# A hybrid encoder block on one core: a hand-set TensorE order for the SSD stage, with the z projection two groups wide

## The chip, the cores and the metric

One core of one Trainium2 chip runs the whole block for one sequence. The time is device microseconds of one execution, as the median of several. Five engines run side by side, each through its own instructions in order: TensorE (PE; its weight loads, PEld, overlap the matmuls), VectorE (DVE), ScalarE (ACT), GpSimd (POOL) and SyncE (SP, which here only issues transfers; its queue stands in the trace as SPq).

## The reference

One layer on x of 512 tokens by 1024, all float32:

```python
h = rms_norm(x)
q, k, v, z, xbc, dt_raw, gates = split(h @ w_in)
attn = diff_attention(q, k, v) @ w_attn_out
ssd = bi_ssd(xbc, dt_raw, z) @ w_ssm_out
x = x + (sigmoid(gate_attn) * attn + sigmoid(gate_ssd) * ssd) @ w_out
x = x + conv_glu(rms_norm(x))
```

The part in question is `bi_ssd`. It works on xBC after a depthwise convolution over 4 tokens and SiLU, in 8 groups of 4 heads of 64 columns, with a state of 128, forward and backward, in chunks of 128 tokens:

```python
acs = cumsum(dt * a)                              # within a chunk; backward from the end
decay = exp(where(mask, acs[l] - acs[s], -inf))
y = (C B^T * decay) @ (x * dt) + exp(acs) * (C @ state)
state = state * exp(acs[-1]) + B^T @ (x * dt * exp(acs[-1] - acs))
y = rms_norm((y_fwd + y_bwd + d_skip * x) * silu(z))     # per group of 256 columns
```

## The kernel before

Every large product is made of three passes over halves: `mm3` (L200) multiplies high by high, high by low and low by high, so a matmul of 128 rows of K is three instructions (L201, L202, L203). The halves `whi` and `wlo` of a weight are made on the chip: the `raw` tile comes by a transfer that SP issues (L133), ACT casts it (L149 for row chunks, L169 for column chunks), and DVE subtracts (L150, L170). `feat` makes features by tokens, 512 tokens wide, so its instructions have 512 columns. `token` makes tokens by features, and for the gate z it is 256 columns wide: one group's z, 4 blocks of 128 tokens, 8 blocks of K, three passes.

The program runs through attention (to about 300 us), the SSD stage (to about 850 us), the output projection and the convolutional MLP. In the attention stage the order on PE is written by hand; `dt_part` (L388 to L447) makes the time step there as fill. It leaves the step `dtk`, the negated sum `acs`, `eacs`, `elast` and `wst` in tokens by heads, and the sums in DRAM as `acsD`.

The SSD stage is emitted by `weave` (L276): `ssd_group(g)`, a generator of five parts, is interleaved with fill, and from what is emitted a scheduler puts each engine's instructions in order. The fill for group g is `ssd_prep(g + 1)`, and for even g from 2 on one part of the output projection, `ssm_out` (L860), behind it. After the loop come the last `base` steps (DVE, transfers) and `ssm_out(3)`.

`ssd_prep(g)` projects B, C and the two halves of x (`feat`), each through `conv_silu` (L709: ACT L711, DVE L712 to L714, ACT tanh L716, DVE L717); turns B into tokens (L729) and makes C B^T (L734), turns x into tokens (L748), and makes the gate z (ACT L754, DVE L755). `ssd_group(g)` does:

- Six contributions to the state, in four turns: POOL weighs x with `wst` (`xw`, L775), PE multiplies (L779, plain float32, bank "av"), and DVE carries the state from chunk to chunk, four heads at a time (L787, L802), or ACT copies it (L790, L792, L795).
- Then four chunks. The row sums of both directions are spread over the partitions by a transfer on SP's queue (`E`, L809, 512 KB). POOL masks them (L813), ACT takes the exponent, 8 heads and directions (L817), ACT scales the backward half by the step (L821), DVE scales the forward half and adds (L822, into `W`), and DVE multiplies with C B^T (L823). POOL starts y with the skip (L825). PE multiplies W with x (L830) and C with the state (L834), DVE adds both (L836, L841) and the gate (L843), ACT sums the squares (L845).
- At the end of the group DVE makes the reciprocal root (L113 to L119) and scales y (L848), PE transposes it (L853), and ACT and DVE split it into halves (L855, L856).

The PSUM banks of the stage are `mm=3, lg=2, ta=1, av=1, tq=1`.

## Time and profile before

| | us |
|---|---|
| median of 3 runs | 1253.79 (1253.76, 1253.79, 1255.59) |
| the profiled execution | 1255.38 |
| its span | 1253.7 |
| PE busy | 1236.6 (99%) |
| DVE busy | 846.0 (67%) |
| ACT busy | 646.1 (52%) |
| POOL busy | 170.4 (14%) |

The profile is of one execution. Its time is 1.7 us above its span and 1.6 us above the median. PE's granted clock was 0.999 of full speed. Busy time of PE is modelled: matmuls overlap, so a row's duration is longer than what the instruction costs, and the cost is the distance from one start to the next.

### The profile page before, as it was taken

The page shows a single profiled execution, that of the slowest core. Times are in us where ns is not written, and L with a number is a line of the kernel's source. Part 1 is how long each engine was busy: PE and PEld are TensorE (multiplying, and loading weights), DVE is VectorE, ACT ScalarE, POOL GpSimd, SP SyncE. Part 2 cuts the span into 40 slices and gives each one's busy share as a digit, 9 for nine tenths or more (in the row PEclk, how much of TensorE's full clock was granted, in tenths as well). Part 3 has the DMA queues.
Part 4 walks back from the last instruction along what each step waited for, and adds up shares of the span by engine and source line. Part 5 has one row for each costly group of instructions (what it writes and reads, how often), then busy time and mean ns, then how long its engine had stood idle before and what let it go on. Part 6 is the DMA issues. An engine that isn't in the chain of part 4 may idle for free.

```text
span 1253.7 us, 18646 instructions
## 1 busy us (share of the span) xinstructions
PE 1236.6 (99%) x6856; PEld 1055.9 (84%) x6856; DVE 846.0 (67%) x1764; ACT 646.1 (52%) x1463; POOL 170.4 (14%) x224
## 2 busy tenths in 40 slices
PE   9989999999999999999999999999999999999998
PEld 7989999888888888888888788878888888888887
DVE  5594757654637989779879788786476666763222
ACT  5574857666525767666556654244344444442111
POOL 3221112101020321203211320041000000000000
PEclk9999999999999999999999999999999999999999
DMA  7231222214434433443243434444133333233331
GB/s 215 83 116 54 81 68 71 78 52 149 136 114 122 126 94 102 119 121 129 86 119 105 133 102 118 134 139 147 34 101 101 101 102 100 91 96 100 109 124 36
DMA packets 112589, 131.86 MB, mean 105 GB/s; under 512 B 4809, under 2 KB 96457, under 8 KB 112498
## 3 DMA queue, kind: packets, MB, share of 16 engines
q1 hardware_dynamic: 112498, 130.67, 33.8%
q8 instruction: 54, 0.88, 0.3%
q14 instruction: 37, 0.30, 0.1%
HBM read 126.30 MB, written 4.36 MB: 104 GB/s over the span
## 4 chain that ended last, share of the span: by engine, by line
PE 81%; DVE 9%; ACT 4%; DMA 3%; issue 2%; POOL 1%; SPq 0%; POOLq 0%; DVEq 0%; ACTq 0%
PE mm L201 22%; PE mm L203 21%; PE mm L202 21%; DMA E<-acsD 2%; PE t L551 2%; PE lg L830 1%; PE lg L834 1%; PE lg L516 1%; ACT E L817 1%; PE av L779 1%; DVE wlo L170 1%; DVE lg L529 1%; PE t L542 1%; PE lg L203 1%; PE lg L202 1%
## 5 line engine op out<-in xcount | busy, mean ns | idle before, releaser
L170 DVE TENSOR_TENSOR wlo<-raw,whi 128x512 fp32r<-128x512 f32 x236 | 162.2, 714 | 93.5 <-ACT whi L169 87.7
L203 PE MATMUL mm<-yo,wlo 128*128 128x512 f32 (+2 forms) x552 | 215.4, 390 | 1.8 <-DVE wlo L170 1.8
L201 PE MATMUL mm<-yo,whi 128*128 128x512 f32 (+1 forms) x552 | 214.6, 391 | 0.0
L202 PE MATMUL mm<-yo,whi 128*128 128x512 f32 (+2 forms) x552 | 213.7, 387 | 0.0
L169 ACT CAST whi<-raw 128x512 fp32r<-128x512 f32 x236 | 136.6, 617 | 125.5 <-PE mm L202 96.1
L201 PE MATMUL mm<-whi,h 128*128 128x256 f32 x640 | 189.8, 297 | 0.7 <-ACT h L259 0.4
L203 PE MATMUL mm<-whi,h 128*128 128x256 f32 x640 | 185.0, 289 | 0.0
L202 PE MATMUL mm<-wlo,h 128*128 128x256 f32 x640 | 184.0, 288 | 0.0
L201 PE MATMUL mm<-h,whi 128*128 128x512 f32 x392 | 158.1, 403 | 0.0
L203 PE MATMUL mm<-h,wlo 128*128 128x512 f32 x392 | 157.1, 401 | 0.0
L202 PE MATMUL mm<-h,whi 128*128 128x512 f32 x392 | 155.4, 396 | 0.0
L150 DVE TENSOR_TENSOR wlo<-raw,whi 128x1024 fp32r<-128x1024 f32 x61 | 74.9, 1228 | 100.5 <-ACT whi L149 100.4
L201 PEld LDWEIGHTS mm<-whi,h 128*128 128x128 f32 x640 | 123.3, 193 | 5.2 <-issue 3.2
L202 PEld LDWEIGHTS mm<-wlo,h 128*128 128x128 f32 x640 | 123.5, 193 | 1.7 <-issue 1.4
L203 PEld LDWEIGHTS mm<-whi,h 128*128 128x128 f32 x640 | 123.1, 192 | 1.5 <-issue 1.2
L203 PEld LDWEIGHTS mm<-yo,wlo 128*128 128x128 f32 x552 | 103.7, 188 | 23.8 <-DVE wlo L170 2.7
L201 PEld LDWEIGHTS mm<-yo,whi 128*128 128x128 f32 x552 | 103.5, 188 | 21.7 <-issue 1.0
L202 PEld LDWEIGHTS mm<-yo,whi 128*128 128x128 f32 x552 | 103.7, 188 | 21.2 <-issue 0.5
L149 ACT CAST whi<-raw 128x1024 fp32r<-128x1024 f32 x62 | 65.0, 1049 | 99.4 <-PE lg L203 39.4
L817 ACT ACTIVATE E<-E,acs 128x128 f32<-128x128 f32 x256 | 81.2, 390 | 62.6 <-POOL E L813 62.6
L203 PEld LDWEIGHTS mm<-h,wlo 128*128 128x128 f32 x392 | 73.6, 188 | 17.8 <-issue 2.4
L201 PEld LDWEIGHTS mm<-h,whi 128*128 128x128 f32 x392 | 73.7, 188 | 16.1 <-issue 2.3
(248 smaller groups left out, 2188.8 us busy)
## 6 DMA issues: line engine op xcount, KB each, us to landing
raw<-in_w_in_dram SPq DMA_DIRECT2D x74, 512.0 KB
raw<-in_w_up_dram SPq DMA_DIRECT2D x44, 512.0 KB
E<-acsD SPq DMA_DIRECT2D x32, 512.0 KB
raw<-in_w_down_dram SPq DMA_DIRECT2D x22, 512.0 KB
raw<-in_w_in_dram SPq DMA_DIRECT2D x32, 256.0 KB
raw<-in_w_ssm_dram SPq DMA_DIRECT2D x16, 512.0 KB
yb<-in_x_dram SPq DMA_DIRECT2D x8, 512.0 KB
raw<-in_w_attn_dram SPq DMA_DIRECT2D x8, 512.0 KB
```

What stands on the lines that cost most here:

```text
L149: A.copy(hi, raw)
L150: (G if k0 in share else V).tensor_tensor(lo, raw, f(hi), SUB)
L169: A.copy(hi[:, k0:k0 + n, :], src)
L170: V.tensor_tensor(lo[:, k0:k0 + n, :], src, f(hi[:, k0:k0 + n, :]), SUB)
L201: PE.matmul(ps, lhsT=lhi, rhs=rhi, start=first, stop=False)
L202: PE.matmul(ps, lhsT=lhi, rhs=rlo, start=False, stop=False)
L203: PE.matmul(ps, lhsT=llo, rhs=rhi, start=False, stop=last)
L516: PE.matmul(lgs[qb - qb0][m], lhsT=a[mp, qs], rhs=b[mp, :], start=(i == 0), stop=(i == 2))
L529: V.tensor_tensor_reduce(lg, ps, bias[:, qb * P:qb * P + T], 1.0, 3.0e38, ADD, MIN, mn[:, m:m + 1])
L542: PE.transpose(ps[:, kb * P:(kb + 1) * P], probs[h, qb][:, kb * P:(kb + 1) * P], ident)
L551: PE.matmul(po, lhsT=at[:, kb * P:(kb + 1) * P], rhs=vt[:, kb, hh * P:(hh + 1) * P], start=(kb == 0), stop=(kb == NT - 1))
L817: A.activation(E[:, d, h, :], E[:, d, h, :], AF.Exp, bias=acs[:, c, s:s + 1])
```

## The change

It rewrites the SSD stage and leaves the arithmetic of the other stages as it was, but for three instructions in `dt_part`.

- **The order on PE.** Within the stage it is written by hand (`direct`): a planner with a clock in microseconds takes the first of the steps "bt" (B to tokens and C B^T), "xt" (x to tokens, and the `xw` of the group), "st" (states), "y" (a chunk) and "yt" (y to features) whose due time has come, and otherwise one piece of fill. The due times are in the diff. Fill is a list of projections, `attn_out`, `ssd_prep`, `z_gate`, `ssm_out`, `gate_ssd`, and at the end the last steps and `ssm_out(3)`.
- **z** is projected for two groups at a time, 512 columns wide, into four "mm" banks at once, from weights in row chunks of two blocks of K.
- **The step in the exponent.** `dt_part` takes the logarithm of the step (DVE maximum, ACT Ln, DVE subtraction), so that the bias of the exponent holds log dt minus the sum. The scaling of both halves (L821, L822) goes; one DVE addition of the two halves (128x512) for each chunk comes in its place. The product with C B^T is made in `E` itself. There is no `W` tile any more, so `E` is held until the chunk's matmuls are done.
- **The transfer of E** is issued by GpSimd in place of SyncE, after the matmuls of the chunk two before.
- **The states** are made in one block: one `xw` tile of six, six matmuls in a row, then two copies and 16 carries on DVE.
- `yz` has one buffer in place of two, and the PSUM banks are `mm=4, lg=2, t=2`.

```diff
-        V.tensor_scalar(acs, acs, -1.0, None, MUL)
+
+        V.tensor_scalar(dtk, dtk, 1.0e-37, None, MAX)
+        A.activation(dtk, dtk, AF.Ln)
+        V.tensor_tensor(acs, dtk, acs, SUB)
...
-    open_banks("psum2", mm=3, lg=2, ta=1, av=1, tq=1)
+    open_banks("psum2", mm=4, lg=2, t=2)
...
+        def z_gate(g):
+
+            for i in range(2):
+                szs[g + i] = ap.tile([P, NT, CW], F32, tag="sz", bufs=3, name=nm("sz"))
+            pss = [bank("mm") for _ in range(NT)]
+            for k0 in range(0, KD, 2):
+                w = RowChunk([w_in_v[:, k0:k0 + 2, C_Z + g * CW:C_Z + (g + 2) * CW]], 2, HW)
+                for tb in range(NT):
+                    for kt in range(k0, k0 + 2):
+                        mm3(pss[tb], hT.h(kt, tb * P, P), hT.l(kt, tb * P, P), w.h(kt - k0), w.l(kt - k0),
+                            kt == 0, kt == KD - 1)
+                        yield 0.68
+                    if k0 == KD - 2:
+                        for i in range(2):
+                            sz, ps = szs[g + i][:, tb, :], pss[tb][:, i * CW:(i + 1) * CW]
+                            A.activation(sz, ps, AF.Tanh, scale=0.5)
+                            V.scalar_tensor_tensor(sz, sz, 1.0, ps, ADD, MUL)
+                yield "block"
+            done["z", g] = done["z", g + 1] = now[0]
...
+        def decay(i):
+
+            if i >= GROUPS * NT:
+                return
+            g, c = divmod(i, NT)
+            E = decays[i] = ap.tile([P, 2, GH, P], F32, tag="E", bufs=2, name=nm("E"))
+            G.dma_start(E.rearrange("p d h l -> p (d h l)"),
+                        acsD[g, c].rearrange("(o d) h l -> o (d h l)", o=1).to_broadcast([P, 2 * GH * P]))
+
+            for d, sgn in ((0, 1), (1, -1)):
+                G.affine_select(out=E[:, d], in_=E[:, d], pattern=[[0, GH], [sgn, P]], compare_op=ALU.is_ge,
+                                fill=-1.0e30, base=0, channel_multiplier=-sgn)
+                for h in range(GH):
+                    s = d * 32 + g * GH + h
+                    A.activation(E[:, d, h, :], E[:, d, h, :], AF.Exp, bias=acs[:, c, s:s + 1])
+            V.tensor_tensor(E[:, 0], E[:, 0], E[:, 1], ADD)
...
+        CONTRIB = ((0, 0), (3, 1), (1, 0), (1, 1), (2, 0), (2, 1))
...
+            xw = ap.tile([P, 6, CW], F32, tag="xw", bufs=1, name=nm("xw"))
+            for i, (c, d) in enumerate(CONTRIB):
+                G.tensor_tensor(heads(xw[:, i, :]), heads(xtok[:, c, :]),
+                                hv(wst, c, d, g).unsqueeze(2).broadcast_to([P, GH, 64]), MUL)
...
+            pa, p1, p2 = bank("t"), bank("lg"), bank("lg")
+            PE.matmul(pa[:, :CW], lhsT=btok[:, 0, :], rhs=xw[:, 0, :], start=True, stop=True)
+            PE.matmul(pa[:, CW:], lhsT=btok[:, 3, :], rhs=xw[:, 1, :], start=True, stop=True)
+            for ps, c in ((p1, 1), (p2, 2)):
+                PE.matmul(ps, lhsT=btok[:, c, :], rhs=xw[:, 2 * c:2 * c + 2, :].rearrange("p d q -> p (d q)"),
                           start=True, stop=True)
...
+            A.copy(S[:, 1, :], pa[:, :CW])
+            A.copy(S[:, 4, :], pa[:, CW:])
+            carry(S[:, 2, :], S[:, 4, :], 2, 1, p2[:, CW:])
+            carry(S[:, 0, :], S[:, 2, :], 1, 1, p1[:, CW:])
+            carry(S[:, 3, :], S[:, 1, :], 1, 0, p1[:, :CW])
+            carry(S[:, 5, :], S[:, 3, :], 2, 0, p2[:, :CW])
...
-                W = ap.tile([P, GH, P], F32, tag="W", bufs=2, name=nm("W"))
-                for h in range(GH):
-                    s = h0 + h
-                    A.activation(E[:, 1, h, :], E[:, 1, h, :], AF.Copy, scale=dtk[:, c, 32 + s:33 + s])
-                    V.scalar_tensor_tensor(W[:, h, :], E[:, 0, h, :], dtk[:, c, s:s + 1], E[:, 1, h, :], MUL, ADD)
-                V.tensor_tensor(W, W, cb[:, c, :].unsqueeze(1).broadcast_to([P, GH, P]), MUL)
...
+        def weigh(i):
+
+            if i < GROUPS * NT:
+                g, c = divmod(i, NT)
+                W = decays[i][:, 0]
+                V.tensor_tensor(W, W, ctxs[g][2][:, c, :].unsqueeze(1).broadcast_to([P, GH, P]), MUL)
...
+            STEPS = {"bt": (b_tokens, 1.4, GROUPS), "xt": (x_tokens, 0.9, GROUPS), "st": (states, 2.6, GROUPS),
+                     "y": (chunk, 1.6, GROUPS * NT), "yt": (y_out, 0.9, GROUPS)}
+            NEVER = 1.0e9
+            nxt = dict.fromkeys(STEPS, 0)
+            clock, t_used = 0.0, -9.0
...
+                if step == "bt":
+                    t = max(after("bc", i, 7.5), after("st", i - 2, 0.0), after("y", NT * (i - 1) - 1, 0.0))
+                elif step == "xt":
+                    t = max(after("x", i, 7.5), after("bt", i, 0.0), after("st", i - 1, 0.0),
+                            after("y", NT * (i - 1) - 1, 0.0))
+                elif step == "st":
+                    t = max(after("bt", i, 4.0), after("xt", i, 7.5), after("y", NT * i - 1, 3.5))
+                elif step == "y":
+                    g, c = divmod(i, NT)
+                    return max(after("st", g, 6.5), after("y", i - 1, 8.5), after("z", g, 2.0),
+                               after("yt", g - 1, 0.0), after("w", i, 4.0))
+                else:
+
+                    t = max(after("y", NT * i + NT - 1, 9.0), after("o", i // 2, 0.0))
+                return max(t, t_used + 2.5)
...
+                step = next((x for x in STEPS if ready[x] <= clock), None)
+                if step:
+                    i = nxt[step]
+                    STEPS[step][0](i)
+                    if step == "y":
+                        decay(i + 2)
...
-        for g in range(GROUPS):
-            fill = [ssd_prep(g + 1)] if g + 1 < GROUPS else [gate_ssd()]
-            n = 6 if g + 1 < GROUPS else 8
-            if g >= 2 and g % 2 == 0:
-                fill.append(ssm_out(g // 2 - 1))
-                n += 4
-            weave(ssd_group(g), chain(*fill), n / 5)
...
+        attn, first = attn_out(), ssd_prep(0)
+        order = [blocks(first, 2), blocks(attn, 1), first, blocks(attn, 1), z_gate(0), blocks(attn, 2)]
+        for g in range(GROUPS):
+
+            order.append(ssd_prep(g + 1) if g + 1 < GROUPS else gate_ssd())
+            if g == 0:
+                order.append(attn)
+            elif g % 2 == 0:
+                order.append(ssm_out(g // 2 - 1))
+            elif g + 1 < GROUPS:
+                order.append(z_gate(g + 1))
+        order += [bases(), ssm_out(3, finish)]
+        with tc.manual_schedule(engines={mybir.EngineType.PE}):
+            direct(chain(*order))
```

Lines after the change: `E` transfer L807, masks L811, exponent L815, addition L816, B to tokens L825, C B^T L828, x to tokens L845, `xw` L849, states L858 to L861, carries L868, skip L888, chunk L894 and L898, y L899 to L908, product with C B^T L915, y to features L926.

On PE, at the start of a z projection, before (group 1; L202 and L203 of `mm_4546` are the end of x's second half, `mm_4647` is z):

```order
L202 MATMUL mm_4546<-h_86,whi_4461 128x512
L203 MATMUL mm_4546<-h_84,wlo_4462 128x512
L201 MATMUL mm_4647<-whi_4636,h_83 128x256
L734 MATMUL ta_4445<-bc_4383,bc_4306 128x128 x4
L202 MATMUL mm_4647<-wlo_4637,h_83 128x256
L203 MATMUL mm_4647<-whi_4636,h_85 128x256
L201 MATMUL mm_4647<-whi_4636,h_83 128x256
L202 MATMUL mm_4647<-wlo_4637,h_83 128x256
L834 MATMUL lg_4423<-S_4225,bc_3707 128x512
```

And after (groups 2 and 3; `mm_4930` is the end of x's second half, `mm_5017` the first of the four z banks):

```order
L202 MATMUL mm_4930<-h_86,whi_4891 128x512
L203 MATMUL mm_4930<-h_84,wlo_4892 128x512
L201 MATMUL mm_5017<-whi_5023,h_83 128x512
L202 MATMUL mm_5017<-wlo_5024,h_83 128x512
L203 MATMUL mm_5017<-whi_5023,h_85 128x512
L201 MATMUL mm_5017<-whi_5023,h_83 128x512
```

The instructions of z are 512 columns wide, and begin right behind the x half. Before, transposes and steps of chunks lay between them.

On DVE, the carries of group 5's states (`S`), before:

```order
L787 SCALAR_TENSOR_TENSOR S_7343<-S_7343,elast,av_7357 128x64 x4
L856 SCALAR_TENSOR_TENSOR yo_7328<-tq_7329,pp,yo_7327 128x512
L170 TENSOR_TENSOR wlo_7580<-raw_7569,whi_7579 128x512
L836 TENSOR_TENSOR yz_7432<-yz_7432,lg_7461 128x256
L822 SCALAR_TENSOR_TENSOR W_7634<-E_7618,dtk 128x128 x4
L170 TENSOR_TENSOR wlo_7580<-raw_7571,whi_7579 128x512
L712 SCALAR_TENSOR_TENSOR bc_7424<-mm_7399,pp,bc_7424 128x511
L823 TENSOR_TENSOR W_7634<-W_7634,cb_6802 128x512
L713 SCALAR_TENSOR_TENSOR bc_7424<-mm_7399,pp,bc_7424 128x510
L787 SCALAR_TENSOR_TENSOR S_7343<-S_7343,elast,av_7367 128x64 x8
L714 SCALAR_TENSOR_TENSOR bc_7424<-mm_7399,pp,bc_7424 128x511
L856 SCALAR_TENSOR_TENSOR yo_7328<-tq_7336,pp,yo_7327 128x512
L802 SCALAR_TENSOR_TENSOR S_7343<-S_7343,elast 128x64 x4
```

And after:

```order
L816 TENSOR_TENSOR E_6764<-E_6764 128x512
L868 SCALAR_TENSOR_TENSOR S_6828<-S_6828,elast,lg_6831 128x64 x4
L915 TENSOR_TENSOR E_6764<-E_6764,cb_6590 128x512
L868 SCALAR_TENSOR_TENSOR S_6828<-S_6828,elast,lg_6830 128x64 x3
L781 TENSOR_TENSOR yb_5703<-mm_6821,yb_5703 128x512
L868 SCALAR_TENSOR_TENSOR S_6828<-S_6828,elast,lg_6830 128x64 x5
L170 TENSOR_TENSOR wlo_6974<-raw_6967,whi_6973 128x512
L170 TENSOR_TENSOR wlo_6974<-raw_6970,whi_6973 128x512
L868 SCALAR_TENSOR_TENSOR S_6828<-S_6828,elast,lg_6831 128x64 x2
L929 SCALAR_TENSOR_TENSOR yo_6895<-t_6896,pp,yo_6894 128x512
L868 SCALAR_TENSOR_TENSOR S_6828<-S_6828,elast,lg_6831 128x64 x2
```

Twelve carries on PE's results and four on the state alone (L802), with instructions of other steps between them, are now sixteen on PE's results. L816 is the new addition, L915 the product with C B^T; L170 and L781 belong to fill, L929 to the y of the group before.

On POOL, around the transfers of E, before (those stand on SP) and after:

```order
L813 AFFINE_SELECT E_4878<-E_4878 128x512 x2
L775 TENSOR_TENSOR xw_4246<-xtok_4021,wst 128x256 x2
L813 AFFINE_SELECT E_4953<-E_4953 128x512 x2
L813 AFFINE_SELECT E_5062<-E_5062 128x512 x2
L813 AFFINE_SELECT E_5141<-E_5141 128x512 x2
L775 TENSOR_TENSOR xw_4788<-xtok_4621,wst 128x256
```

```order
L849 TENSOR_TENSOR xw_4574<-xtok_4561,wst 128x256 x6
L888 TENSOR_TENSOR yz_4745<-xtok_4561,rows 128x256 x4
L807 DMA E_4763<-acsD 128x1024
L811 AFFINE_SELECT E_4763<-E_4763 128x512 x2
L807 DMA E_4852<-acsD 128x1024
L811 AFFINE_SELECT E_4852<-E_4852 128x512 x2
L807 DMA E_4977<-acsD 128x1024
L811 AFFINE_SELECT E_4977<-E_4977 128x512 x2
L807 DMA E_5076<-acsD 128x1024
```

Each transfer now stands in POOL's own row, behind the mask of the chunk before, and the first of a group behind the six `xw` and four skip products.

## Rows read from the trace of the kernel before

**Rows 1.** Busy us (count) of each engine in two windows; clock, DMA share, GB/s
```profile
300.00:820.00 520.00, 517.80 (x2822) 439.71 (x2821) 409.54 (x996) 298.48 (x764) 99.49 (x143) 1.00 0.38 116
820.00:850.00 30.00, 27.67 (x118) 21.25 (x117) 27.58 (x28) 15.40 (x21) 14.63 (x8) 1.00 0.60 188
```

**Rows 2.** Groups of PE instructions, 300 to 820 us: busy, mean ns | idle before
```profile
L203 PE MATMUL mm<-h,wlo 128*128 128x512 f32 x317 | 127.6, 403 | 0.0
...
L203 PE MATMUL mm<-whi,h 128*128 128x256 f32 x256 | 75.0, 293 | 0.0
...
L203 PE MATMUL mm<-yo,wlo 128*128 128x512 f32 x166 | 66.5, 400 | 0.0
...
L830 PE MATMUL lg<-xtok,W 128*128 128x64 f32 x256 | 33.3, 265 | 0.0
L834 PE MATMUL lg<-S,bc 128*128 128x512 f32 x32 | 16.4, 594 | 0.0
...
L748 PE MATMUL tq<-ident,xf 128*128 128x128 f32 x64 | 10.6, 272 | 0.0
L834 PE MATMUL lg<-S,bc 128*128 128x256 f32 x32 | 9.8, 389 | 0.3 <-DVE S L802 0.3
...
L734 PE MATMUL ta<-bc,bc 128*128 128x128 f32 x64 | 9.1, 275 | 0.0
```

**Rows 3.** PE in order of time, 384 to 392 us: start, duration, instruction
```profile
384.85 0.39 PE L201 MATMUL mm<-h,whi 128*128 128x512 f32 x1
385.07 1.02 PE L779 MATMUL av<-xw,btok 128*128 128x512 f32 x2
...
386.17 0.40 PE L203 MATMUL mm<-h,wlo 128*128 128x512 f32 x1
386.40 0.40 PE L201 MATMUL mm<-h,whi 128*128 128x512 f32 x1
...
391.65 0.39 PE L203 MATMUL mm<-h,wlo 128*128 128x512 f32 x1
```

**Rows 4.** PE in order of time, from 404.5 us
```profile
407.38 0.28 PE L203 MATMUL mm<-whi,h 128*128 128x256 f32 x1
407.50 0.28 PE L201 MATMUL mm<-whi,h 128*128 128x256 f32 x1
```

**Rows 5.** Groups of DVE instructions, 290 to 845 us: busy, mean ns | idle
```profile
L822 DVE SCALAR_TENSOR_TENSOR W<-E,dtk 128x128 f32<-128x128 f32 x128 | 47.2, 416 | 5.4 <-ACT E L821 5.4
...
L823 DVE TENSOR_TENSOR W<-W,cb 128x512 f32<-128x512 f32 x32 | 22.4, 701 | 0.5 <-ACT cb L736 0.3
```

**Rows 6.** The same of ACT
```profile
L821 ACT ACTIVATE E<-E,dtk 128x128 f32<-128x128 f32 x128 | 43.2, 392 | 0.0
```

**Rows 7.** The table load of ACT: count, duration min/median/max in ns, start us
```profile
L296 ACT ACT_TABLE_LOAD  x1: 1283/1283/1283, 0.8 to 0.8; - x1
```

**Rows 8.** ACT in order of time, 128 to 133 us
```profile
132.07 0.72 ACT L532 ACTIVATE lg<-lg,mn 128x512 f32<-128x512 f32 x1 [1.92 <-DVE mn L529]
```

**Rows 9.** DVE in order of time, 770 to 778 us, carries of group 7
```profile
772.64 1.62 DVE L787 SCALAR_TENSOR_TENSOR S<-S,elast,av 128x64 f32<-128x64 f32 x8
...
776.03 0.87 DVE L802 SCALAR_TENSOR_TENSOR S<-S,elast 128x64 f32<-128x64 f32 x4
```

**Rows 10.** SP's queue, 565 to 573 us: a transfer of E is issued
```profile
568.43 0.34 SPq L809 DMA_DIRECT2D E<-acsD  x1
```

**Rows 11.** POOL in order of time, the mask on that E
```profile
572.18 1.22 POOL L813 TENSOR_SCALAR_AFFINE_SELECT E<-E 128x512 f32<-128x512 f32 x2 [4.49 <-DVE yz L841]
```

**Rows 12.** Waits, 290 to 845 us: total us, times, longest us
```profile
ACT E L817 <- POOL E L813: 62.6, 29, 8.9
...
DVE rsv L113 <- ACT ysq L845: 8.0, 5, 3.0
```

**Rows 13.** ACT in order of time, 669 to 671 us: a convolution begins
```profile
669.49 0.78 ACT L711 ACTIVATE xf<-mm,pp 128x512 f32<-128x512 f32 x1
```

**Rows 14.** DVE in order of time: the same convolution's last read of PSUM, and its end
```profile
676.30 0.75 DVE L714 SCALAR_TENSOR_TENSOR xf<-mm,pp,xf 128x511 f32<-128x511 f32 x1
...
679.97 0.68 DVE L717 SCALAR_TENSOR_TENSOR xf<-th,xf 128x512 f32<-128x512 f32 x1
```

275 lines of the change are left out of this document (145 added, 130 removed).

## The prediction

> **What bounds the kernel now.** I read the busy times by window first. From 300 to 820 us, nearly all of the SSD stage, PE is busy 517.80 of 520 us at a granted clock of 1.00; DVE has 409.54, ACT 298.48, POOL 99.49 [rows 1]. PE is the bound, so only two things shorten the stage: cheaper instructions on PE, or fewer waits of PE. The last 30 us differ: PE 27.67, DVE 27.58 [rows 1], so there the two wait for each other.
>
> Busy time is modelled, so I made a second count of PE's waits from the distances of starts. From 386.40 to 391.65 us lie 23 steps of 512 columns: 0.228 us each [rows 3]. Two neighbours of 256 columns lie 0.12 apart [rows 4]. From 384.85 to 386.17 run two of 512 columns and one plain float32 product of 512, which so costs 1.32 - 0.46 = 0.86 [rows 3]. The groups give the counts [rows 2]: 317+316+316 and 169+166+166 matmuls of 512 columns (one line of each three stands), 1450 × 0.228 = 331; 3 × 256 of z, 768 × 0.12 = 92.2; the rest, from counts of records (two to a float32 matmul): 32 × 0.86, 32 × 0.44, 128 × 0.22, 156 transposes × 0.11 and 32 × 0.22 make 94. Together 517.2, so PE lost 2.8 us in 520. In the tail 118 × 0.228 = 26.9, so 3.1 of 30 lost [rows 1]. **All waits that the new order could remove are 5.9 us.**
>
> **z, 512 columns wide.** 768 instructions of 256 columns become 384 of 512: 92.2 → 384 × 0.228 = 87.6. All of it lies on PE, which is the bound: **-4.6**. The multiplied numbers and the weights' bytes are the same.
>
> **The logarithm.** DVE gets one instruction more, hidden: DVE is no bound in attention. ACT gets Ln, between two table loads, since the exponent follows. A load took 1.283 [rows 7], Ln is some 0.4 by the 0.392 of an ACT instruction [rows 6], together 3.0; where it stands ACT sat idle for 1.92 [rows 8], so ACT comes 1.0 late, once. Between 0 and 1.0 reaches PE, whose order there has other work: **+0.5**. The Trainium skill ("ScalarE: Activation LUTs", What ACT_TABLE_LOAD costs) puts a drain of about 1.38 us behind each load; by that ACT would be 3.8 late and the term 1.9, the sum 1.4 higher. No row here shows the drain.
>
> **Work off DVE and ACT.** L821 goes, 43.2 us of ACT [rows 6]; L822 goes, 47.2 of DVE, and 32 additions of 128x512 come, at the 0.70 of L823 22.4 [rows 5]: DVE -25, ACT -43 in the stage. None of it is on PE's path now, so it is worth nothing by itself. It pays for shorter chains, on which the hand-set order relies.
>
> **The order on PE.** The waits of before go with the old order: **-5.9**. The new order has fixed distances, and PE waits wherever a chain is longer than the matmuls that were put between. Worked out from the new order with the costs above, four places are tight.
>
> - z's banks. z takes all four "mm" banks; the fourth is that of x's second half, just ended. 18 matmuls stand between: 4.1 us. The convolution must have read the bank by then: in one crowded case that took from 669.49 to 676.30 + 0.7, 7.5 us [rows 13, 14]; alone it is one ACT and three DVE instructions, some 3.3 with the hand-over. It occurs with a chunk beside it in groups 2, 4 and 6. Between 0 and 3.4 each; nearer to the free one, as DVE has less work: 0.7 each, **+2**.
> - States to the first chunk. In groups 1, 3, 5, 7 only 27 matmuls and 8 transposes stand between, 27 × 0.228 + 8 × 0.11 = 7.0 us; in the others 9.6 or more. On DVE, 16 carries at 1.62/8 = 0.20 [rows 9] are 3.2; in groups 3, 5 and 7 five instructions of other steps stand among or just ahead of them, at some 0.6 to 0.7 (0.70 is L823's, [rows 5]), 3.1; ACT's two copies and hand-overs ahead, 1.0. Together 7.3. Below, nothing (if the first chunk waits only for its own eight carries); above, 1.5 each, if DVE is behind. **+2** for the three.
> - Last chunk to y's transposes: 28.7 us in group 0, then 14.4 to 9.1. The chain is DVE, ACT's squares, the reciprocal root, the scaling; DVE already waited 8.0 us in five cases for the squares [rows 12]. 0 to 8; three of the eight are at 9.1 to 10.2: **+1.5**.
> - The tail keeps its last chain (DVE was as busy as PE [rows 1]): half of the 3.1, **+1.5**.
>
> **The transfer of E** goes from SP's queue to POOL. From its issue at 568.43 to the mask at 572.18 were 3.75 us [rows 10, 11]; with the mask's 1.22 [rows 11], eight exponents of 0.32 and two DVE instructions of 0.7, about 9. It is issued when the chunk two before has ended; chunks stand some 10 us apart, so there are about 20: **0**, with 11 us of cover. SP's queue, which loads the weights, gets free of a wait that held it.
>
> **The sum**: -4.6 + 0.5 - 5.9 + 2 + 2 + 1.5 + 1.5 = **-3.0**. The profiled execution took 1255.38 (span 1253.7, 1.7 around it), 1.6 above the median of 1253.79; the differences hold for either, so 1250.8 against the median. 0.2% is 2.5 us, about what a measurement can tell.
>
> **Rivals.**
>
> *All distances suffice* (A). DVE has 25 us less to do and the transfers come early; then only the tail waits: -4.6 + 0.5 - 5.9 + 1.5 = -8.5, **1245.3**. For it: most distances are 8 to 14 us. Against it: the four places above, and that a fixed order cannot give way when a chain is late.
>
> *Convolutions as slow as before* (C; slower). From x's second half to its transposes the new order has 7.5 to 8.2 us, from B and C 8.2 to 13.7. The chain shown, from ACT's first instruction at 669.49 to DVE's last at 679.97 + 0.68, took 11.2 [rows 13, 14]. Of the 32 chains of before half are over 8 us, since DVE and ACT have other steps in front; if those lengths stayed, the excess would sum to 22 us. A wait of PE lets the others catch up, so about half would show: +11 less the 2 that z's banks have already: 1250.8 + 9 = **1260**. It decides when a chain with other steps in front passes 8 us. Against it: those lengths grew with the old mixing, and L821 and L822 stood in them.
>
> *E comes late from POOL* (B; slower). ACT stands in order: the exponents wait for the mask (62.6 us in 29 cases [rows 12]), and behind them the casts and the convolutions' first reads. On POOL the issue stands behind six `xw` products and four skips. Were each E 2 us later for ACT, the sixteen B/C and x steps, whose distance is their chain's, would each lose about 0.7: +11, **1262**. It decides from 11 us of lateness for the chunk itself, but at once for what stands behind on ACT. The Trainium skill ("SBUF — State Buffer", SBUF: two separate sides) warns of this: descriptors of a transfer issued by GpSimd are written by GpSimd, and DVE instructions of some kinds lock it out; it advises SP or ACT as the issuer. No row of before shows a transfer from POOL.
>
> *The change doesn't do what it says*: PE stays as full as it was, z alone counts, waits neither go nor come: -4.6 + 0.5 = -4.1, 1249.7. This falls into the forecast's own range.
>
> **How the numbers follow.** Forecast 0.47, own range 1247.5 to 1254.5 (ends of the four places); A 0.18; C 0.12; B 0.12; the rest 0.11, on both sides. The range 1243.5 to 1262 takes in A with 2 us below it, and C and B. Faster by over 0.2% (under 1251.3): a little over half of the forecast, A and half of the rest, 0.49. Within 0.2%: 0.24. Slower: C, B and a bit, 0.27.
>
> **What will show it.** z's groups must be 384 instructions of 512 columns and 256-column z gone. PE's idle time must be named by DVE (S, carries) at L894 in odd groups, by z's fourth bank at L201 to L203, by DVE at L926. If PE waits at L845 or L825 for DVE's end of a convolution, it is C; if at L898 for E, or if ACT's wait for POOL's mask at L815 grows past 62.6 us, B. If PE's waits in the stage sum to under 3 us, A. Wrong altogether would be a 512-column z matmul at over 0.24 us, or a granted clock under 1.00.

## The result: slower by 1.2%

| | before | after |
|---|---|---|
| median, us | 1254.69 | 1269.75 (1266.34 to 1272.29, 4 runs) |
| ratio, with 95% interval | | 1.0123 [1.0104, 1.0142] |
| the profiled execution; its span | 1255.38; 1253.7 | 1272.03; 1270.3 |
| mean granted clock | 0.999 | 0.993 |

The forecast was 1250.8, in a range of 1243.5 to 1262. The long window of [rows 1] in the changed kernel, with the same columns:

```profile
300.00:820.00 520.00, 504.65 (x2381) 411.27 (x2380) 387.21 (x884) 261.80 (x624) 117.54 (x170) 0.99 0.36 114
```

PE now stands idle for 15.4 us, where it was 2.2 in [rows 1], although DVE is busy 22 us less in this window and ACT 37 less. To see where the time lies I made for both kernels the count that the prediction made for one window: the distances of starts on PE, against the cost of each instruction by its spacing at the full clock. SSD and the output projection stand together, since ten matmuls of the one now stand among those of the other. The times count from PE's first matmul, and the loss is that of the profiled execution.

| PE, us | before: time | lost | after: time | lost |
|---|---|---|---|---|
| to the last attention matmul | 291.3 | 19.3 | 295.4 | 23.2 |
| SSD and output projection | 594.7 | 9.6 | 607.3 | 27.0 |
| the MLP | 361.7 | 0 | 361.7 | 0 |

The work of the middle row fell from 585.1 to 580.3. The losses rose by 17.4 there and by 3.9 in attention. Of the latter 1.2 stand ahead of any instruction that was changed: PE's last transpose of the time step (L441) comes 122.0 us behind PE's first matmul before, 123.2 after, and from 119.5 to 124.4 in the runs below, which all have the same instructions up to there.

z did what was said. One of the three lines of its matmuls, where [rows 2] has 256 columns:

```profile
L201 PE MATMUL mm<-whi,h 128*128 128x512 f32 x128 | 52.8, 413 | 3.6 <-DVE xf L719 3.6
```

What PE waited for, over the whole span (total us, times, longest us):

```profile
PE t L545 <- ACT osq L558: 6.0, 4, 2.0
PE t L828 <- DVE bc L722: 5.4, 2, 3.0
PE mm L201 <- DVE xf L719: 3.6, 3, 2.7
PE lg L898 <- issue: 3.0, 3, 1.3
PE t L845 <- DVE xf L722: 1.7, 2, 1.0
...
PE t L926 <- DVE yz L921: 1.5, 1, 1.5
```

Only L545 belongs to attention. The others are in the SSD stage and are all of the kind that the prediction named: a convolution's end (L828, L845), its last read of the bank that z takes next (L201), a first chunk (L898), the scaling of y (L926).

**One of the long ones, on three engines.** PE at the B and C step of group 2, then ACT and DVE in the same stretch:

```profile
453.03 2.08 PE L828 MATMUL t<-bc,bc 128*128 128x128 f32 x8 [2.45 <-DVE bc L722]
454.90 1.78 PE L894 MATMUL lg<-S,bc 128*128 128x512 f32 x2
```

```profile
442.72 0.78 ACT L716 ACTIVATE bc<-mm,pp 128x512 f32<-128x512 f32 x1
...
446.62 2.46 ACT L815 ACTIVATE E<-E,acs 128x128 f32<-128x128 f32 x8 [1.06 <-POOL E L811]
...
450.59 0.62 ACT L721 ACTIVATE th<-bc 128x512 f32<-128x512 f32 x1
```

```profile
446.50 0.75 DVE L719 SCALAR_TENSOR_TENSOR bc<-mm,pp,bc 128x511 f32<-128x511 f32 x1
449.16 0.69 DVE L816 TENSOR_TENSOR E<-E 128x512 f32<-128x512 f32 x1 [1.92 <-ACT E L815]
449.89 0.69 DVE L915 TENSOR_TENSOR E<-E,cb 128x512 f32<-128x512 f32 x1
...
452.30 0.68 DVE L722 SCALAR_TENSOR_TENSOR bc<-th,bc 128x512 f32<-128x512 f32 x1
```

PE stands for 2.45 us until 453.0, for the end of C's convolution (L722, 452.30). That convolution was read out of its bank by 447.2, and its tanh (L721) could have begun then. But ACT's row has the eight exponents of a chunk's E ahead of it (446.62, after a wait of 1.06 for POOL's mask), then a weight cast and the next convolution's first step. DVE's row has the addition of E's halves (L816, after 1.92 of waiting for those exponents), the product with C B^T (L915), a weight half and the next convolution's first sum ahead of L722. Both engines had just stood idle; what holds them is a fixed row, in which a convolution stands behind E. The convolution's chain took 10.3 us from 442.72, against 8.2 that the order gives. The two longer waits have the same rows: at 690.28 (2.98 us, L828) the exponents begin at 683.48, after 1.79 of waiting for the mask, and the tanh at 687.84; at 581.29 (2.68 us, z's bank) the exponents begin at 574.96, after 2.87, and DVE stands for 4.06 for a weight cast behind them.

**The clock behind it.** Windows of 2 us; the last number but two is the granted clock:

```profile
452.00:454.00 2.00, 0.97 (x4) 0.97 (x5) 1.97 (x4) 0.00 (x0) 0.00 (x0) 0.75 0.50 128
454.00:456.00 2.00, 2.00 (x8) 1.48 (x7) 0.42 (x1) 0.85 (x2) 0.00 (x0) 0.50 0.45 135
```

PE works on, at half the clock from about 453 to past 456: the product L894, 0.86 at the full clock, took 1.6. Of the five waits of PE of 1.9 us and more in this profile, three (1.99, 2.45 and 2.68 us, ending at 148, 453 and 581) were followed by such a stretch; two (1.92 us, ending at 79, and 2.98, ending at 690) were not. Two more such stretches, at 16 and at 98 us, stand in attention; the one at 98, behind a wait of 1.47, is in the kernel before too.

**States to first chunk.** In group 5, PE, then DVE:

```profile
661.24 0.59 PE L894 MATMUL lg<-S,bc 128*128 128x256 f32 x2
663.16 1.08 PE L898 MATMUL lg<-xtok,E 128*128 128x64 f32 x8 [1.33 <-issue]
```

```profile
656.23 0.69 DVE L816 TENSOR_TENSOR E<-E 128x512 f32<-128x512 f32 x1 [3.06 <-ACT E L815]
...
662.60 0.46 DVE L868 SCALAR_TENSOR_TENSOR S<-S,elast,lg 128x64 f32<-128x64 f32 x2
```

The first product of the chunk (L894) starts in time, so the state that it reads is ready. The second (L898) starts 0.1 us behind the very last carry, which ends at 663.06; in groups 3 and 7, where it waits too, it is the same 0.1. It reads nothing of the states; but the program gives it one of the two "lg" banks that held their products, and that is what I take it to wait for (no run gives it a bank of its own). The first carry began late, because L816 stands ahead of it and waited 3.06 for the exponents.

### The profile page after: what moved, and what is told of

Same layout as the page of the kernel before. It is cut to its first block, busy times and chain, and to the rows that moved or that the text cites. A ratio compares the mean times of both kernels' runs of the same rounds, so it can differ in the third digit from the quotient of the medians.

```text
span 1270.3 us, 17629 instructions
## 1 busy us (share of the span) xinstructions
PE 1238.6 (98%) x6472; PEld 1040.4 (82%) x6472; DVE 832.2 (66%) x1669; ACT 614.3 (48%) x1330; POOL 191.7 (15%) x256
## 4 chain that ended last, share of the span: by engine, by line
PE 81%; DVE 7%; issue 5%; ACT 4%; DMA 1%; POOL 1%; SPq 0%; POOLq 0%; DVEq 0%; ACTq 0%
PE mm L201 22%; PE mm L202 22%; PE mm L203 22%; PE lg L898 2%; PE t L554 2%; PE lg L894 1%; ACT lg L535 1%; PE lg L861 1%; DVE lg L532 1%; DVE wlo L150 1%; ACT E L815 1%; PE lg L519 1%; PE t L545 1%; PE t L202 1%; PE t L201 1%
## 5 line engine op out<-in xcount | busy, mean ns | idle before, releaser
L170 DVE TENSOR_TENSOR wlo<-raw,whi 128x512 fp32r<-128x512 f32 x236 | 162.8, 721 | 87.8 <-ACT whi L169 79.7
L201 PE MATMUL mm<-yo,whi 128*128 128x512 f32 (+1 forms) x552 | 215.5, 392 | 0.0
L203 PE MATMUL mm<-yo,wlo 128*128 128x512 f32 (+2 forms) x552 | 213.6, 387 | 0.0
L202 PE MATMUL mm<-yo,whi 128*128 128x512 f32 (+2 forms) x552 | 213.4, 387 | 0.0
L201 PE MATMUL mm<-whi,h 128*128 128x256 f32 (+1 forms) x512 | 168.1, 329 | 3.6 <-DVE xf L719 3.6
L203 PE MATMUL mm<-whi,h 128*128 128x256 f32 (+1 forms) x512 | 161.5, 315 | 0.0
L202 PE MATMUL mm<-wlo,h 128*128 128x256 f32 (+1 forms) x512 | 160.7, 314 | 0.0
L201 PE MATMUL mm<-h,whi 128*128 128x512 f32 x392 | 156.9, 400 | 0.0
L203 PE MATMUL mm<-h,wlo 128*128 128x512 f32 x392 | 153.2, 391 | 0.0
L202 PE MATMUL mm<-h,whi 128*128 128x512 f32 x392 | 152.8, 390 | 0.0
L150 DVE TENSOR_TENSOR wlo<-raw,whi 128x1024 fp32r<-128x1024 f32 x61 | 75.0, 1229 | 105.1 <-ACT whi L149 105.1
L202 PEld LDWEIGHTS mm<-yo,whi 128*128 128x128 f32 x552 | 103.7, 188 | 21.4 <-issue 1.0
L201 PEld LDWEIGHTS mm<-yo,whi 128*128 128x128 f32 x552 | 103.5, 188 | 21.7 <-issue 1.0
L203 PEld LDWEIGHTS mm<-yo,wlo 128*128 128x128 f32 x552 | 103.6, 188 | 21.0
L201 PEld LDWEIGHTS mm<-whi,h 128*128 128x128 f32 x512 | 99.9, 195 | 11.2 <-issue 6.3
L202 PEld LDWEIGHTS mm<-wlo,h 128*128 128x128 f32 x512 | 100.1, 196 | 5.6 <-issue 1.0
L203 PEld LDWEIGHTS mm<-whi,h 128*128 128x128 f32 x512 | 99.7, 195 | 5.5 <-DVE h L260 0.2
L815 ACT ACTIVATE E<-E,acs 128x128 f32<-128x128 f32 x256 | 79.1, 389 | 46.1 <-POOL E L811 46.1
L203 PEld LDWEIGHTS mm<-h,wlo 128*128 128x128 f32 x392 | 73.6, 188 | 15.9
L201 PEld LDWEIGHTS mm<-h,whi 128*128 128x128 f32 x392 | 73.7, 188 | 14.5 <-issue 0.7
```

The source lines that it names most:

```text
L150: (G if k0 in share else V).tensor_tensor(lo, raw, f(hi), SUB)
L170: V.tensor_tensor(lo[:, k0:k0 + n, :], src, f(hi[:, k0:k0 + n, :]), SUB)
L201: PE.matmul(ps, lhsT=lhi, rhs=rhi, start=first, stop=False)
L202: PE.matmul(ps, lhsT=lhi, rhs=rlo, start=False, stop=False)
L203: PE.matmul(ps, lhsT=llo, rhs=rhi, start=False, stop=last)
L815: A.activation(E[:, d, h, :], E[:, d, h, :], AF.Exp, bias=acs[:, c, s:s + 1])
```

## The experiments

All times are medians, each beside the kernel before on the same chip (1254.2 to 1255.0). "Lost" is PE's loss in SSD and output projection by the count above: 9.6 before, 27.0 after. It belongs to the profiled execution, which can lie some us from the median (that of the change took 1272.0, the one with the distance 12.0 below took 1260.2).

### Distances in the hand-set order

```diff
-                    t = max(after("bc", i, 7.5), after("st", i - 2, 0.0), after("y", NT * (i - 1) - 1, 0.0))
+                    t = max(after("bc", i, 10.5), after("st", i - 2, 0.0), after("y", NT * (i - 1) - 1, 0.0))
...
-                    t = max(after("x", i, 7.5), after("bt", i, 0.0), after("st", i - 1, 0.0),
+                    t = max(after("x", i, 10.5), after("bt", i, 0.0), after("st", i - 1, 0.0),
```

> The changed kernel with the planner's distance from a convolution's projection to its transposes (B and C to L825 and L828, x to L845) 10.5 in place of 7.5; nothing else. Theory 1: the main loss is that the exponents of E stand in ACT's row ahead of a convolution's tanh, so that the chain is 7 to 10 us long and PE waits at L828 and L845 (8.1 us by the distances of starts, and some 2 us at the half clock behind the longest): these go, about 1259.5. Rival: a chain that is late shifts the whole group, and the waits come back at the next steps (L858, L894, L926): 1268 to 1270, the waits named there.

1261.9 (ratio 1.0057 [1.0036, 1.0078]), lost 21.3. The 7.8 us at L828 and L845 are gone, as theory 1 says. But others came up, as the rival says: 4.4 at L926 in place of 1.7, 3.0 at L858 in place of nothing, and 1.9 behind z, for z's own banks. The time lies between the two.

```diff
-                    return max(after("st", g, 6.5), after("y", i - 1, 8.5), after("z", g, 2.0),
+                    return max(after("st", g, 9.5), after("y", i - 1, 8.5), after("z", g, 2.0),
```

> The changed kernel with the distance from the states to the group's first chunk 9.5 in place of 6.5. Theory: L898 of the first chunk waits for the last of the 16 carries, since its bank is one of those that hold the states' products (0.73, 1.49 and 1.31 us in groups 3, 5 and 7): these go, about 1266.3. Rival: the chunks come later, and the wait moves to L926 or to the end of the stage: no change within 1 us.

1258.1 (1.0024 [1.0011, 1.0037]), lost 15.5. This is 11.7 off, three times the waits that it was made for. The 3.5 us at L898 went, and with them the 5.8 at L828 and 1.7 at L926, which I had not connected. Neither theory had that.

Both edits together:

> The changed kernel with both distances longer: convolution to transposes 10.5 in place of 7.5, states to first chunk 9.5 in place of 6.5. Theory: what the first alone left (L898 1.9 us, L201 behind the carries, L858) is the states' bank, and what the second alone left (L845 0.7) is the convolution; together they leave some 4 us less than the second alone: 1254 to 1256. Rival: any shift only moves where the chains of a group collide (the first alone made new waits at L926 and L858 of 1.8 and 0.8 to 1.3): 1258 to 1262.

1284.2 (1.0243 [1.0209, 1.0278]), lost 39.9: the worst of all, above both ranges, though every distance is at least as long as in the change. What PE waits for there:

```profile
PE mm L201 <- DVE xf L719: 9.9, 3, 3.9
PE mm L201 <- DVE sz L760: 6.6, 3, 3.1
```

Now z waits for the last half of x, and the projection behind z for z's own banks.

The same line as in the second, with 12.0 and with 8.0:

> The changed kernel with the states' distance 12.0 (6.5 as changed, 9.5 in the third experiment, 1258.1 us). Theory 4: the distance itself had been too short, and beyond 9.5 nothing more is gained: 1257 to 1260. Rival: it is the phase that counts, at which the chunks fall on the convolutions, and 12.0 is another phase: over 1263 or under 1254.

> The changed kernel with the states' distance 8.0 (6.5: 1269.8, 9.5: 1258.1, 12.0: 1266.0). Theory 4 (distance): 7.3 was the chain, so 8.0 is enough and gives nearly all that 9.5 gave: 1258 to 1262. Rival (phase): the time follows where chunks and convolutions fall together, and 8.0 may be anywhere from 1255 to 1280, with waits at places other than L898.

12.0 gave 1266.0 (1260.2 to 1268.5; 1.0089 [1.0062, 1.0115]), lost 20.0. 8.0 gave **1252.6** (0.9983 [0.9969, 0.9996]), lost 9.5, below both ranges. So 6.5, 8.0, 9.5 and 12.0 give 1269.8, 1252.6, 1258.1 and 1266.0. The wait at L898 is gone from 8.0 on, which is distance. That the time rises again beyond it is the rival's phase, the place where the chunks fall between the convolutions: with 12.0, PE waits at L845 and behind z. The same convolution as above, C of group 2, with 8.0, on ACT and on POOL:

```profile
437.45 0.77 ACT L716 ACTIVATE bc<-mm,pp 128x512 f32<-128x512 f32 x1
441.85 0.63 ACT L721 ACTIVATE th<-bc 128x512 f32<-128x512 f32 x1 [3.64 <-DVE bc L719]
...
446.17 1.28 ACT L815 ACTIVATE E<-E,acs 128x128 f32<-128x128 f32 x4 [1.11 <-POOL E L811]
```

```profile
439.89 0.55 POOL L807 DMA_DIRECT2D E<-acsD  x1 [5.72 <-PE lg L898]
444.81 1.91 POOL L811 TENSOR_SCALAR_AFFINE_SELECT E<-E 128x512 f32<-128x512 f32 x2 [4.37 <-DMA E<-acsD]
```

The chunk of before now ends on PE at 439.4, 1.9 us behind the convolution's start (437.45), where it had ended 1.5 ahead of it (441.2 against 442.72). E's transfer starts at a chunk's end, its mask 4 to 5 us later; so the mask comes at 444.81, behind the tanh at 441.85, and the chain is 6.2 us in place of 10.3. Over the whole stage 2 of the 32 convolutions take more than 8 us from ACT's first instruction to DVE's last, where the change has 5 and the kernel before had 17.

### Where E comes from

```diff
-            G.dma_start(E.rearrange("p d h l -> p (d h l)"),
+            SY.dma_start(E.rearrange("p d h l -> p (d h l)"),
```

> The changed kernel with the transfers of E issued by SyncE again; nothing else. Theory: E is 9.5 us and more ahead of its matmuls in every chunk, so the queue is worth nothing by itself: 1268 to 1271 (a shift of the collisions may move it by 3). Rival (the prediction's B): issuing from GpSimd makes the masks and exponents late and these hold ACT: 1260 or less, and ACT's wait for the mask (46.1 us) clearly shorter.

1279.7 (1.0204 [1.0173, 1.0235]), lost 42.3. Ten us worse, which neither theory had; so the move to POOL's queue had been a gain in this order. The mask's wait for the transfer was 118.9 in the changed kernel; here it is:

```profile
POOL E L811 <- DMA E<-acsD: 301.9, 30, 22.2
```

SyncE's row stands for 87.0 us for the chunks that free E's buffer (19 times), and the transfer in turn stands among the weights.

```diff
-            E = decays[i] = ap.tile([P, 2, GH, P], F32, tag="E", bufs=2, name=nm("E"))
+            E = decays[i] = ap.tile([P, 2, GH, P], F32, tag="E", bufs=3, name=nm("E"))
```

> The changed kernel with three buffers of E in place of two; nothing else. Theory 2: E's transfer can only be issued when the chunk two before has left PE, so that mask and exponents come when ACT and DVE have already reached them in their rows, and both stand there (ACT 46.1 us for the mask, DVE 33.0 us for the exponents) with a convolution or a weight cast behind; with a third buffer E comes a chunk earlier: both waits under half, PE's losses in the SSD stage from 22.9 to 10 or less, 1255 to 1260. Rival: the fixed distances of the order are too short by themselves, E or not: waits at L828, L201 and L898 as before, 1266 to 1272.

```diff
-            V.tensor_tensor(E[:, 0], E[:, 0], E[:, 1], ADD)
+            W = wts[i] = ap.tile([P, GH, P], F32, tag="W", bufs=2, name=nm("W"))
+            V.tensor_tensor(W, E[:, 0], E[:, 1], ADD)
```

> The changed kernel with the separate W tile of the kernel before (two buffers): the sum of the halves goes to W, so that E is free after that addition and not after the chunk's matmuls. Theory 2: as with a third buffer of E, since E is free some 10 us earlier: 1255 to 1261. Rival: as above, 1266 to 1272.

1269.3 (1.0117 [1.0100, 1.0133], lost 24.7) and 1273.1 (1.0152 [1.0134, 1.0170], lost 29.1). Theory 2 falls. The third buffer shows why, on PE and POOL:

```profile
442.66 1.00 PE L898 MATMUL lg<-xtok,E 128*128 128x64 f32 x8
```

```profile
444.19 0.55 POOL L807 DMA_DIRECT2D E<-acsD  x1 [4.24 <-issue]
448.34 1.22 POOL L811 TENSOR_SCALAR_AFFINE_SELECT E<-E 128x512 f32<-128x512 f32 x2 [3.60 <-DMA E<-acsD]
```

E does come a chunk earlier for its own matmuls (at least 21 us ahead in place of 11). But what lets a transfer go is still the end of some chunk on PE (443.7, issue at 444.19), so the mask and the exponents fall at the same place between the chunks and the convolutions. More buffers change which chunk E is for, hardly when ACT gets it.

Three buffers, 9.5, and the late logarithm (below):

> Three buffers of E, the states' distance of 9.5 and the logarithm at the end of the attention stage together. Theory 2: with E early the convolutions' waits that the longer distance removed by a shift are gone at their cause, so the rest of the losses in the stage falls under 8 us: 1250 to 1253. Rival: each shift makes new collisions (as both lags together did): 1255 to 1260.

1259.0 (1.0032 [1.0020, 1.0045]), lost 18.5: 4.3 slower than without the third buffer (1254.6, below). The rival.

```diff
-                                fill=-1.0e30, base=0, channel_multiplier=-sgn)
-                for h in range(GH):
+                                fill=-1.0e4, base=0, channel_multiplier=-sgn)
+                for h in range(0, GH, 2):
```

> The changed kernel with four of the eight exponents of each chunk left out (and a smaller mask value, so that all stays finite): the decay is then wrong, all else is done. Theory 3: the exponents' 2.45 us stand in ACT's row ahead of a tanh or a weight cast, so the chains are that much shorter: PE's losses at L828, L845 and z fall by half (11.9 to about 6), 1260 to 1264. Rival: the distances are too short without them, or the collisions only shift: 1267 to 1273.

This leaves out half of the exponents. 1264.0 (1.0081 [1.0066, 1.0097]), lost 20.6, at the edge of theory 3. L828 and L845 lost 3.3 in place of 7.8, z 5.2 in place of 4.1, L898 nothing. The exponents are a part of the chains, but taking half away shifts others too; by itself this does not show how much is theirs.

### z

z's first two row chunks for three banks, then both for the fourth:

```diff
+            for k0, tbs in ((0, (0, 1, 2)), (2, (0, 1, 2)), (0, (3,)), (2, (3,)), (4, range(NT)), (6, range(NT))):
```

> The changed kernel, with the fourth bank of z left out of z's first two row chunks and made behind them, so that 36 matmuls (8.2 us) and not 18 (4.1 us) stand ahead of the first use of the bank that x's second half has just left. Theory: PE's waits for L719 at z's start (2.84, 0.68 and 0.58 us) and the half clock behind the first (1.8 us) go: about 1264. Rival: the transfer and the halves of the next weights come no earlier, so PE waits there instead: 1268 to 1270.

1269.8 (1.0119 [1.0090, 1.0148]), lost 28.5. z's waits of 4.1 are gone, and nothing is gained: 2.6 at L858, and 2.5 more in the output projection, appeared. The rival's time, by another way.

```diff
...
-            pss = [bank("mm") for _ in range(NT)]
+            for i in range(2):
+                w = RowChunk([wcols(w_in_v, C_Z + (g + i) * CW)])
...
+                    ps = yield from token_steps(w, hT, tb)
```

> The changed kernel with z 256 columns wide again, one bank at a time, inside the new hand-set order. Theory: PE pays 4.6 us, z's waits for its banks (4.1) and the half clock behind one of them (1.8) go, the waits at L828 and L898 stay: 1268 to 1270. Rival: the block of four banks is what sets the order's phases, and one bank at a time is worth more: 1262 or less.

1276.7 (1.0178 [1.0161, 1.0195]): 6.9 worse, above both ranges. PE pays the 4.6, and waits 8.0 for the halves of z's weights (L150), which were 4.1 for banks.

The kernel before, with z 512 wide by the same four-bank code and the banks of the change (the share of fill for each group was fitted to it):

> The kernel before with one part of the change: z 512 columns wide for two groups, four banks at once (banks mm=4, lg=2, t=2); the scheduler still sets PE's order. Theory: the 4.6 us of PE come whole, since a scheduler's order can put other matmuls where z would wait for its banks: 1249 to 1251.5. Rival: the four banks cost by themselves what they save, by whoever sets the order: 1254 to 1257.

1260.5 (1.0052 [1.0037, 1.0067]), lost 21.1: slower also where a scheduler sets the order, and above both ranges. One wait alone:

```profile
PE t L861 <- DVE yz L856: 5.5, 1, 5.5
```

This is the last group's y, near 820 us. As I read it, z of groups 6 and 7 is made together and early, so the last groups have less fill beside their chains; no run shows that. What else it lost (8 us in small pieces) I have not followed up.

### The logarithm

```diff
-        A.activation(dtk, dtk, AF.Ln)
+        A.copy(dtk, dtk)
```

> The changed kernel with Ln in the time step's part replaced by a copy, which needs no table: the decay is then not the reference's, all work but the two table loads is. Theory: the attention stage, 4.1 us longer than before, loses the wait at the table loads (1.3 us more of idle time of PE at 146 us) and the half clock behind it (1.7 us): about 1266.7, and no clock below 1.00 at 148 to 154 us. Rival: the stage's extra time is the chance of one execution, and the time stays at 1269 to 1270.

This leaves out the logarithm and with it the two table loads. 1265.0 (1.0079 [1.0051, 1.0108]), 4.8 less. Attention as a whole does not show it, since it began slowly here (L441 at 124.4 us); behind L441 it does: from there to the last attention matmul are 169.5 us, where the change has 172.2 and the kernel before 169.3.

The states' distance of 9.5, with the logarithm at the end of attention (an addition of a zero that is made from the last gate keeps it there):

```diff
+    V.tensor_scalar(late, gate_a[3][:, 1, 0:1], 0.0, None, MUL)
+    V.tensor_scalar(dtk, dtk, 1.0e-37, late, MAX, ADD)
+    A.activation(dtk, dtk, AF.Ln)
+    V.tensor_tensor(acs, dtk, acs, SUB)
```

> The changed kernel with the states' distance of 9.5, and the logarithm of the time step made at the end of the attention stage, behind its last gate, in place of the middle of it; results as the reference's. Theory: the two table loads cost 3 to 4.8 us where ACT's softmax stands behind them, and nothing at the stage's end, where the first chunk is 70 us away: 1253.5 to 1255. Rival: the attention stage is longer by chance of the run, or the loads hold up the first casts and convolution of the next stage just as much: 1257 to 1259.

1254.6 (1.0000 [0.9988, 1.0013]): 3.5 less than with the distance alone; from L441 to the last attention matmul are 169.4 us, as before the change.

Then the kernel before with this part of the change alone, first with the logarithm as in the change, then at the end of attention:

```diff
-                    A.activation(E[:, 1, h, :], E[:, 1, h, :], AF.Copy, scale=dtk[:, c, 32 + s:33 + s])
-                    V.scalar_tensor_tensor(W[:, h, :], E[:, 0, h, :], dtk[:, c, s:s + 1], E[:, 1, h, :], MUL, ADD)
+                V.tensor_tensor(W, E[:, 0], E[:, 1], ADD)
```

> The kernel before with one part of the change: log of the time step in the exponent, the addition of the halves into W in place of L821 and L822. Theory: it takes 43 us off ACT and 25 off DVE, but PE lost only some 6 us to waits there; it gains at most 4 and pays 3 to 5 for the table loads: 1253 to 1257. Rival: DVE and ACT are what sets the stage, and the relief is worth more: 1248 or less.

> The kernel before with the log of the time step in the exponent (as in the eighth experiment, 1256.4), and the logarithm made at the end of the attention stage. Theory: the eighth kernel lost 6.6 us in the SSD stage (8.1 before) and paid 1.1 us in the attention stage and 1.5 in the output projection; without the table loads in the middle of attention the first goes: 1253 to 1255. Rival: the loads at the stage's end hold up its successor's first casts: 1256 to 1258.

1256.4 (1.0016 [1.0004, 1.0028]) and 1254.2 (0.9995 [0.9981, 1.0009]). By the count the relief of DVE and ACT is worth some 1.5 us of losses in the SSD stage in both, and the output projection loses 1.5 to 2 more, so that no gain is left; the table loads in the middle of attention cost 2.2 on top.

### Both mends together

The states' distance of 8.0 and the late logarithm:

> The changed kernel with the states' distance of 8.0 (1252.6) and the logarithm at the end of the attention stage. Theory: the table loads' 3 us come off as with the distance of 9.5 (1258.1 to 1254.6): 1249 to 1250.5, faster than the kernel before by 0.3 to 0.4%. Rival: moving the logarithm shifts the first chunks, and the phase takes the gain back: 1252 to 1256.

**1250.2** (1248.8 to 1251.2; 0.9966 [0.9952, 0.9979]): faster than either kernel, and 19.5 us less than the change: 17.1 by the distance and 2.4 more by the place of the logarithm. (Alone on the change, without the loads, the second was 4.8; that the two add up is not shown.) The longest of PE's waits, and the first window, where the change had 504.65:

```profile
PE t L541 <- ACT osq L554: 4.6, 4, 1.9
PE mm L201 <- DVE xf L720: 1.8, 3, 1.0
```

```profile
300.00:820.00 520.00, 517.46 (x2461) 423.70 (x2460) 404.66 (x908) 269.27 (x635) 119.00 (x172) 1.00 0.37 117
```

SSD and output projection take 590.1 with 9.9 lost, where before had 594.7 with 9.6: what is left of the change is just z's saving. Within that sum the SSD stage loses 2.5 less than before and the output projection 2.8 more. The states in one block and the single `yz` buffer were not run by themselves.

## Why the prediction was wrong

The step that failed is how the waits of the hand-set order were priced. The sum took each tight place by itself and came to 7.0 us, put the convolutions at 0, gave the clock no price, and took 5.9 off for the old waits. Measured in the two stages: 13.4 at the four places, 7.8 at the convolutions, 3.3 in two stretches at half the clock, 24.5 of the 27.0 us lost; and the old waits were not won, since even the best order lost 9.9. One run shows what lies behind it: 1.5 us more of a single distance took 17.1 us off.

- **z, -4.6.** Right: 585.1 to 580.3 of PE's work in the two stages, z's part being 92.2 - 87.6.
- **The logarithm, +0.5.** Too small by a factor of five or six: 2.2, 2.4, 3.5 and 4.8 in four pairs of runs, and 2.9 from L441 to the end of attention (169.3 to 172.2). ACT was late by 1.3 (134.57 against 132.07 in [rows 8], less the 1.2 that this kernel was behind already), where 1.0 was reckoned:

```profile
131.35 1.28 ACT L449 ACT_TABLE_LOAD   x1
132.84 0.42 ACT L449 ACTIVATE dtk<-dtk 128x256 f32<-128x256 f32 x1 [0.21 <-DVE dtk L448]
133.28 1.28 ACT L535 ACT_TABLE_LOAD   x1
134.57 0.73 ACT L535 ACTIVATE lg<-lg,mn 128x512 f32<-128x512 f32 x1
```

The two loads and Ln take 3.2 us, which is 1.28 twice, 0.42, and 0.21 of waiting for DVE. The Trainium skill ("ScalarE: Activation LUTs", What ACT_TABLE_LOAD costs) has a drain of about 1.38 us with each load, 2.66 for a switch, which by estimate would make 5.3 of the two loads and 5.7 with Ln. No such drain stands beside either load in this row. What failed is "PE, whose order there has other work". It has none 14 us on:

```profile
147.85 0.66 PE L545 MATMUL t<-ident,lg 128*128 128x128 f32 x4 [1.99 <-ACT osq L558]
```

and before:

```profile
145.35 0.66 PE L542 MATMUL t<-ident,lg 128*128 128x128 f32 x4 [0.66 <-ACT osq L555]
```

The clock behind the wait, after:

```profile
150.00:152.00 2.00, 2.00 (x11) 2.00 (x11) 1.63 (x3) 0.45 (x2) 0.32 (x1) 0.50 0.85 245
```

The wait was 0.66 and is 1.99, and the clock is at half behind it: 1.3 us of lateness on ACT became three on PE. The half clock is not certain. In the 13 profiles with the loads at this place (the change and twelve runs) the wait is 1.98 to 2.00; in eleven the clock fell behind it, and from L441 on attention took 172.1 to 172.2 us; in two it did not, and it took 170.6. In the seven others the wait is 0.66 to 0.87, and it took 169.3 to 169.5.

- **Waits removed, -5.9.** Not won. In the best order the SSD stage loses 2.5 less than before, and the output projection 2.8 more. The 5.9 itself was low: it was counted with 0.228 a step, where most steps take 0.227, and the later count has 9.6 for the two stages.
- **z's banks, +2.** Measured 4.1 (2.84, 0.68, 0.58), inside the bounds given.
- **States to the first chunk, +2.** Here the failed step shows. The wait itself was 3.5 (0.73, 1.49, 1.31) where 2 was said, and it stood at L898, not at L894 as the prediction has it: the last carry came 8.7 us behind the states in group 5 (7.9 and 8.5 in groups 3 and 7), not 7.3. The sum had counted five instructions of other steps by their durations; six stand there, and one of them, L816, was held for 3.06 by E's exponents. But 1.5 us more distance in the planner gained 17.1 us. I priced a short distance by its own wait alone. In a fixed order it also sets when chunks end, so when E's transfers go, and where on ACT and DVE E's work meets the convolutions. Which distance falls well was tried, not derived: 8.0 is the best of four, 12.0 is bad again. That the mended kernel lands at 1250.2, beside the 1250.8 of the forecast, is luck.
- **Convolutions, 0 in the sum.** 7.8 at L828 and L845. Rival C had the place but not the condition: the chains were not as slow as before, 5 of 32 over 8 us where 17 had been; the two longest, 10.3 and 9.3, made the two waits at L828. Rival B had the way, that lateness of E counts "at once for what stands behind on ACT", but by its own sign it was out: ACT's wait for the mask fell from 62.6 us to 46.1. E was not late by its issuer; it came where the order put it. The Trainium skill ("SBUF — State Buffer", SBUF: two separate sides), with its warning of GpSimd as the issuer, does not decide here: the transfer from GpSimd needed 3.6 to 6.5 us from issue to mask, where SyncE's had needed 3.75 [rows 10, 11], and back on SyncE the kernel was 10 us slower.
- **E itself, 0 with 11 us of cover.** Right: its exponents are done 11.2 us or more ahead of its matmuls. The cover was counted for the matmuls only, not for the rows in which the work stands.
- **y's transposes, +1.5.** Measured 1.7.
- **The tail, +1.5.** The output projection lost 4.1 where it had lost 1.5, and as much in the mended kernels. PE:

```profile
860.74 0.50 PE L202 MATMUL mm<-wol,h 128*128 128x512 f32 x1 [0.80 <-DVE wol L1054]
...
878.72 1.29 PE L252 MATMUL t<-ident,sq 128*128 128x128 f32 x8 [0.69 <-DVE sq L249]
```

Both wait for DVE, as does a third (0.41 at 864.2), which works without a break to 865 us; on it, and on POOL beside it:

```profile
850.91 1.78 DVE L1010 TENSOR_TENSOR h<-yb,h 128x512 fp32r<-128x512 f32 x1
...
857.77 0.68 DVE L1010 TENSOR_TENSOR h<-yb,h 128x512 fp32r<-128x512 f32 x1
```

```profile
850.46 1.67 POOL L1007 TENSOR_TENSOR yb<-yb,yb 128x512 f32<-128x512 f32 x1 [2.36 <-DVE yb L1006]
...
857.93 1.67 POOL L1007 TENSOR_TENSOR yb<-yb,yb 128x512 f32<-128x512 f32 x1 [2.36 <-DVE yb L1006]
```

The same subtraction takes 1.78 us where POOL's addition began ahead of it (850.46 against 850.91), and 0.68 where the addition began behind it (857.93 against 857.77). This lengthens DVE's row, but it is not new: three of these eight subtractions took 1.77 to 1.79 us before, four take 1.77 to 1.79 now. What made the 2.6 us more is open.

- **The clock.** "A granted clock under 1.00" stood among what would make the prediction wrong, without a price. Each half-clock stretch cost 1.6 to 1.7 us: the two in the SSD stage 3.3 of its 17.4, the one at 149 us 1.7 in attention.

## What to carry to other kernels

When an order becomes fixed, a distance that is a little short is not a loss of that little: check what the delayed step triggers (a buffer released, a transfer, a burst on an engine that runs in order), and price what stands behind that burst, not only the step itself. Give such a distance a sweep before the change is judged: here 6.5, 8.0, 9.5 and 12.0 lay 17 us apart, and the change was a loss or a gain by it. Sweep such distances together, too: two that each gained alone lost 14 us together. And put a pair of table loads where nothing that PE awaits is due on the same engine.
